# Depthwise convolution of mixer A: 124 VectorE tap operations become column-tiled TensorE products

## The chip, the cores and the metric

One Trainium2 chip, one NeuronCore of it, fp32 data. The metric is device time of one launch in microseconds (us). The kernel before was run three times: 1407.37, 1408.38 and 1410.26 us, so its median is 1408.38 us. One more execution was taken with the hardware profiler; all rows in this document come from it.

## What is computed

One layer of a hybrid decoder on 320 tokens: 256 of a prompt, then 8 sequences of 8 tokens. Cut to what matters here:

```python
def conformer_conv(a_val, a_gate, conv_prev, conv_w, conv_b, ln_g, ln_b):   # mixer A, 4 heads of 128 channels
    z = a_val * jax.nn.sigmoid(a_gate)
    zp = jnp.concatenate([conv_prev, z], axis=1)                            # 30 earlier tokens of state in front
    y = lax.conv_general_dilated(zp, conv_w[:, None, :], window_strides=(1,), padding="VALID",
                                 feature_group_count=W_A)                   # depthwise, 31 taps
    y = layernorm_heads(y + conv_b, ln_g, ln_b, N_HEADS_A)
    return jax.nn.silu(y), zp[:, -30:]                                      # the new state is an output

h = rmsnorm(x, g_mix); proj = h @ w_in                                      # 2048 x 3072
a_val, a_gate, b_u, b_v, c_u = split(proj)
out_a, conv_new = conformer_conv(a_val, a_gate, ...)                        # mixer A
out_b, v_rows   = chunk_spatial_gate(b_u, b_v, ...)                         # mixer B
out_c, hr, hi   = s5_branch(c_u, ...)                                       # mixer C, complex diagonal recurrence
x = x + concat([out_a, out_b, out_c]) @ w_out
gate, up = split(rmsnorm(x, g_ffn) @ w_gu)
x = x + (silu(gate) * up) @ w_down                                          # then a last RMSNorm
```

For a prompt the 30 earlier tokens are zeros; for the 8 sequences they come from `state_conv`.

## The kernel before

**The main stream.** Channels lie on partitions, tokens in the free dimension. All weights pass TensorE (PE) as *units* of up to 8 chunks of 128 rows. For a unit SP loads 512 KB (`raw`, L194, three buffers; `load(u + 3)` stands at the start of unit u), ScalarE (ACT) makes a rounded copy `hi` (L201), VectorE (DVE) makes the remainder `lo` (L206, a call of the helper at L55; from unit 20 on POOL makes a part of it, L209), and PE does three products per chunk: hi by the high part of the activations (L233), hi by their low part (L234), lo by the high part (L236), 24 of 128x320 per unit. The string `ORDER` sets the sequence of the input projection after heads 0 and 1 of mixer A: `C0` to `C7` are the eight output tiles of mixer C with two units each, `A2` and `A3` the gate and value tiles of heads 2 and 3, `V` the value rows of mixer B, `U0` to `U3` its gates. Then come 16 tiles of `w_out` over the rows of mixer C, 16 over those of mixers A and B, and the feed-forward part. From the end of mixer A and B on PE is busy to the end.

**The side work.** Everything else (convolution, recurrence, gating) is Python generators that the class `Side` hands out in turns between the quarters of a unit, four turns a unit, by priority and by an estimate of DVE's time against PE's. So the order of every engine's instructions is fixed when the program is built; `Wait(n)` means n turns.

**Mixer A.** `post_val` writes z of a head into a padded row `zpad0` or `zpad1` (two DVE operations at L59). `mix_a` (its lines start at L518) lets ACT copy it into `zp`, five blocks of 8 shifted columns (L524, L525), SP store the two new states (L526, L527), and DVE do the 31 taps: one multiply with bias (L65), one multiply (L64), 29 multiply-adds `ac<-zp,cw,ac` (L59) into two accumulators, one add (L55). PE subtracts the mean over channels with the matrix `cent` (L547, result `yc`); `mix_a_tail` gets the variance (PE, L557), the normed value and the activation, and ACT puts it back in token order (L568, L570).

**Mixer C.** POOL computes the parameters of the state space in a long chain of small operations that ends in `kk` (L341 to L445). DVE makes `bb` of them (`bb_task`, the operations `wv<-kk,lnv`). Per tile: `c_inputs` (POOL, L639 to L645) makes powers, PE transposes them (L720), `U` holds the inputs, reordered through DRAM by SP (`du`, L597, and L601), PE makes the states at chunk ends (L708), ACT copies them to `H` (L709). After the fourth tile `recurrence(0)` starts on half of the pairs (copy `F<-H` at L69), after the eighth `recurrence(1)`; each has 63 steps of four DVE operations of 128x32. `c_mats` and `mat_t` make the output matrices with products in four column tiles of the PE array (L820), `c_out` and `c_glu` (L892, L893) the outputs. `w_out` waits for these rows (`need_c`), its second half for all side work (`need_ab`).

Of the kernel before, what the change touches and what calls it, by code (L numbers as in the profile page):

```python
# [40 lines left out]
class Vec:  # L41
    """VectorE with a running estimate of its busy time (us)."""
# [51 lines left out]
class Side:  # L94
    """Side work, handed out between the matrix products of the main stream."""
# [21 lines left out]
    def run(self):  # L117
        """One turn: side work up to VectorE's share of the time that TensorE has been given."""
# [29 lines left out]
def _build(ctx, nc, tc, I, O):  # L148
# [30 lines left out]
    units = []  # L179

    S = {}                 # what the tasks leave for each other

    def unit(src, n, mm, cost, pre=None, post=None):
        units.append(dict(src=src, n=n, mm=mm, cost=cost, pre=pre, post=post))
# [11 lines left out]
    def split_hi(u):  # L196
        if u < len(units):
            d = units[u]
            d["hi"] = wp.tile([128, d["n"]], F32R, tag="hi", name="hi")
            for o in halves(u, d["n"]):  # L200
                A.activation(d["hi"][:, o], d["raw"][:, o], AF.Copy)  # L201

    def split_lo(u):
        if u < len(units):
# [11 lines left out]
    def tile_units(src, rows, post, need=None, psum=acc):  # L216
        """Units of one output tile: ps = W^T act over the chunks that rows() gives."""
# [37 lines left out]
    for _ in range(11):    # TensorE's clock rises with its load  # L255
        T.matmul(wps[:, 0:128], zero, zero, start=True, stop=True)
# [16 lines left out]
    cw = tmp("cw", (128, 4, 31))  # L273
# [10 lines left out]
    # zeroed once: the blocks off the diagonal and the paddings stay zero  # L284
    bds, zpads = [], []
    for i in range(2):
        b_ = tmp(f"zpad{i}", (128, 30 + NT))
        G.memset(b_[:, 0:30], 0.0)
        zpads.append(b_)
# [11 lines left out]
    def inv_sqrt(pool, var, shape, tag, neg, n=1.0):  # L301
        """(var / n + eps)^-1/2, table value and one Newton step; negated if neg. n is a power of 4."""
# [14 lines left out]
    E = G  # L317
# [77 lines left out]
    E.tensor_tensor(sp, sp, fr, op=MULT)          # sin, cos  # L395
    pw = tmp("pw", (128, 2, 5, 32))               # powers 0..4 of abar, re and im
# [26 lines left out]
    def rd_params():  # L423
        # 1 / |a|^2, with one Newton step
# [9 lines left out]
    def k_params():  # L434
        # k = (abar - 1) / a
# [72 lines left out]

    def post_val(h):
# [8 lines left out]
    def mix_a(h):  # L518
# [861 lines left out]
```

## Time and profile before

| what | value |
|---|---|
| runs, us | 1407.37, 1408.38 (median), 1410.26 |
| profiled execution, span, us | 1408.6 |
| mean granted TensorE clock | 0.97 |
| PE busy, us | 1316.6 (93%) |
| DVE busy, us | 816.4 (58%) |
| ACT busy, us | 569.1 (40%) |
| POOL busy, us | 267.8 (19%) |

The span is the time from the first to the last instruction of the profiled execution; the profile gives no other time of it. It lies 0.2 us above the median of the runs. In the rows, L12 is line 12 of the kernel before; `acc<-xh,lo` says that `acc` is written from `xh` and `lo`, with buffer numbers left out. A matrix product in full fp32 shows as two records. PEclk is the granted clock, 1.00 for 2.4 GHz.

### The profile page before, as it was taken

The numbers are of one execution on the slowest core, as the hardware profiler recorded it, in microseconds if no ns is written. First come the engines' busy times: TensorE is split into PE (matmuls) and PEld (weight loads), VectorE is DVE, ScalarE is ACT, GpSimd is POOL, SyncE is SP. The second block draws the span as 40 slices with busy tenths as digits, with TensorE's granted clock in tenths as the row PEclk, the third lists the DMA queues.
The fourth block names the chain that finished last, engine by engine and source line by source line (L and its number), as shares of the span: only waits on it lengthen the run. The fifth ranks groups of instructions, "written<-read, shape, count | busy, mean of one in ns | idle before, by whom it ended". The sixth has DMA issues, their size and how long they took to land.

```text
span 1408.6 us, 22244 instructions
## 1 busy us (share of the span) xinstructions
PE 1316.6 (93%) x8812; PEld 1292.6 (92%) x8812; DVE 816.4 (58%) x1420; ACT 569.1 (40%) x823; POOL 267.8 (19%) x364
## 2 busy tenths in 40 slices
PE   9589678798989999999999999999999999999995
PEld 9588667587889999999999999999999999999995
DVE  7398999989975544444444444444444444444444
ACT  7466434454455533333333333333333333333442
POOL 8775553446533000000000000000000000000112
PEclk9899888999999999999999999999999999999998
DMA  7253234345334444444444444444444444444443
GB/s 258 88 161 123 79 112 127 97 146 194 100 131 152 150 148 152 149 150 147 153 150 150 147 153 150 150 150 150 150 150 149 151 150 149 150 150 142 141 150 122
DMA packets 75369, 203.23 MB, mean 144 GB/s; under 512 B 17616, under 2 KB 27088, under 8 KB 75264
## 3 DMA queue, kind: packets, MB, share of 16 engines
q1 hardware_dynamic: 73472, 195.73, 42.1%
q0 software_dynamic: 1216, 4.41, 1.0%
q8 instruction: 69, 1.13, 0.3%
q10 hardware_dynamic: 576, 1.66, 0.3%
q14 instruction: 36, 0.29, 0.1%
HBM read 194.63 MB, written 7.14 MB: 143 GB/s over the span
## 4 chain that ended last, share of the span: by engine, by line
PE 72%; DVE 4%; DMA 0%; issue 0%; DVEq 0%; ACT 0%; ACTq 0%
PE acc L236 24%; PE acc L234 24%; PE acc L233 24%; DVE ac L59 2%; DVE lo L55 1%; DVE xa L55 1%; DMA xa<-in_xT 0%; DVEq L1376 0%; DVE gs L55 0%; PE sm L547 0%; DVE is L59 0%; PE sm L557 0%; PE sm L1165 0%; PE sm L1099 0%; ACT is L305 0%
## 5 line engine op out<-in xcount | busy, mean ns | idle before, releaser
L55 DVE TENSOR_TENSOR lo<-raw,hi 128x1024 fp32r<-128x1024 f32 (+2 forms) x357 | 410.1, 1150 | 209.6 <-issue 164.4
L201 ACT ACTIVATE hi<-raw 128x1024 fp32r<-128x1024 f32 (+1 forms) x357 | 365.0, 1024 | 328.4 <-PE acc L234 266.1
L233 PE MATMUL acc<-hh,hi 128*128 128x320 f32 x1408 | 424.1, 309 | 0.0
L234 PE MATMUL acc<-hl,hi 128*128 128x320 f32 x1408 | 423.1, 308 | 0.0
L236 PE MATMUL acc<-hh,lo 128*128 128x320 f32 x1408 | 320.9, 308 | 0.0
L234 PEld LDWEIGHTS acc<-hl,hi 128*128 128x128 f32 x1408 | 264.4, 188 | 0.1
L233 PEld LDWEIGHTS acc<-hh,hi 128*128 128x128 f32 x1408 | 264.2, 188 | 0.1
L236 PEld LDWEIGHTS acc<-hh,lo 128*128 128x128 f32 x1408 | 235.0, 188 | 0.0
L233 PE MATMUL acc<-fh,hi 128*128 128x320 f32 x704 | 211.9, 309 | 0.0
L234 PE MATMUL acc<-fl,hi 128*128 128x320 f32 x704 | 211.8, 308 | 0.0
L236 PE MATMUL acc<-fh,lo 128*128 128x320 f32 x704 | 165.5, 308 | 0.0
L1159 POOL COPY ss<-sq 128x320 f32<-128x320 f32 x1 | 0.5, 451 | 852.0 <-ACT sq L1155 852.0
L233 PEld LDWEIGHTS acc<-fh,hi 128*128 128x128 f32 x704 | 132.2, 188 | 0.0
L234 PEld LDWEIGHTS acc<-fl,hi 128*128 128x128 f32 x704 | 132.2, 188 | 0.0
L236 PEld LDWEIGHTS acc<-fh,lo 128*128 128x128 f32 x704 | 119.0, 188 | 0.0
L236 PE MATMUL acc<-xh,lo 128*128 128x320 f32 x288 | 71.1, 330 | 39.8 <-DVE lo L55 39.7
L55 DVE TENSOR_TENSOR xa<-acc,xa 128x320 f32<-128x320 f32 x80 | 39.2, 490 | 107.9 <-PE acc L236 107.9
L233 PE MATMUL acc<-xh,hi 128*128 128x320 f32 x288 | 94.7, 336 | 2.0 <-ACT wv L969 2.0
L209 POOL TENSOR_TENSOR lo<-raw,hi 128x512 fp32r<-128x512 f32 (+1 forms) x44 | 70.6, 1605 | 113.2 <-PE acc L236 24.6
L234 PE MATMUL acc<-xl,hi 128*128 128x320 f32 x288 | 91.2, 324 | 0.0
L236 PEld LDWEIGHTS acc<-xh,lo 128*128 128x128 f32 x288 | 51.7, 203 | 42.3 <-DVE lo L55 42.1
L1143 ACT ACTIVATE fh<-fu 128x320 fp32r<-128x320 f32 x44 | 20.8, 472 | 163.7 <-DVE fu L55 163.7
(297 smaller groups left out, 1624.8 us busy)
## 6 DMA issues: line engine op xcount, KB each, us to landing
raw<-in_wgu SPq DMA_DIRECT2D x176, 512.0 KB, 3.6
raw<-in_wdn SPq DMA_DIRECT2D x80, 512.0 KB, 3.5
raw<-in_win SPq DMA_DIRECT2D x37, 512.0 KB, 3.8
raw<-in_wout SPq DMA_DIRECT2D x32, 512.0 KB, 3.6
raw<-in_wv SPq DMA_DIRECT2D x8, 512.0 KB, 3.5
raw<-in_wdn SPq DMA_DIRECT2D x16, 256.0 KB, 2.7
xa<-in_xT POOLq DMA_DIRECT2D x4, 640.0 KB, 6.7
raw<-in_win SPq DMA_DIRECT2D x6, 256.0 KB, 6.3
```

The costliest lines, as they stand in the source:

```text
L55: return self.v.tensor_tensor(out, a, b, op=op)
L59: return self.v.scalar_tensor_tensor(out, a, s, b, op0=op0, op1=op1)
L201: A.activation(d["hi"][:, o], d["raw"][:, o], AF.Copy)
L209: G.tensor_tensor(d["lo"][:, n:], d["raw"][:, n:], d["hi"][:, n:].bitcast(F32), op=SUB)
L233: T.matmul(ps, hi[:, c], r[u + j][0], start=u + j == 0, stop=False)
L234: T.matmul(ps, hi[:, c], r[u + j][1], start=False, stop=False)
L236: T.matmul(ps, lo[:, j * 128:j * 128 + 128], r[u + j][0], start=False, stop=u + j == n - 1)
L1143: A.activation(h, ub, AF.Copy)
L1159: G.tensor_copy(s, q)
```

## The change

The 31 taps of a head become one unit of the main stream without `hi` and `lo`: `K0` to `K3`. Its 512 KB of weights (`cwd`) hold, for eight groups j of four taps and for four groups g of 32 channels, a 128x32 block whose four 32x32 parts are diagonal, one part per tap. Its input `z4` holds the padded row four times per channel group, shifted by 0 to 3 tokens, so that partitions are (shift, channel). A head then takes 8 x 4 products over the 256 prompt columns and 8 x 4 over the 64 sample columns, each group g into its own column tile of the PE array. The shifted rows are made by writing the padded row (128x596) to DRAM (`zr`, SP) and reading four pieces back (SP); the prompt's and the samples' parts lie in one row with their 30 columns of state in front, which SP now loads from `state_conv` directly into the row. The two output states are stored from the row by POOL's queue.

```diff
-ORDER = "C0 C1 C2 C3 C4 C5 C6 C7 A2 U0 U1 A3 V U2 U3".split()
+ORDER = "C0 C1 K0 C2 C3 K1 C4 C5 C6 C7 A2 U0 U1 K2 A3 V K3 U2 U3".split()
+ZS, ZW, Z4 = 288, 596, 592
 def post_val(h):
     def f(ps):
         side.until(lambda: h < 2 or ("zp", h - 2) in S)
-        z = zpads[h % 2][:, 30:30 + NT]
-        V.scalar_tensor_tensor(z, ps, 0.5, S["rstd"], op0=MULT, op1=MULT)
-        V.scalar_tensor_tensor(z, S["gs", h], 1.0, z, op0=ADD, op1=MULT)
-        side.add(5.5 + 0.1 * h, mix_a(h))
+        row, gs = zpads[h % 2], S["gs", h]
+        V.scalar_tensor_tensor(gs, gs, 1.0, ps, op0=ADD, op1=MULT)
+        V.scalar_tensor_tensor(row[:, 30:286], gs[:, 0:NP], 0.5, S["rstd"][:, 0:NP], op0=MULT, op1=MULT)
+        V.scalar_tensor_tensor(samples(row)[:, :, 30:38], gs[:, NP:]..., 0.5, S["rstd"][:, NP:]..., op0=MULT, op1=MULT)
+        side.add(0.3, conv_in(h))
+def state_load(h):
+    nc.sync.dma_start(samples(zpads[h % 2])[:, :, 0:30], I["sconv"][h].rearrange("p (s t) -> p s t", s=8))
+def conv_in(h):
+    row = zpads[h % 2]
+    dz = dp.tile([128, ZW], F32, tag="zr", name="zr")
+    yield Wait(2)
+    nc.sync.dma_start(dz, row)
+    nc.gpsimd.dma_start(O["ncp"][h], row[:, 256:286])
+    nc.gpsimd.dma_start(O["ncs"][h].rearrange("p (s t) -> p s t", s=8), samples(row)[:, :, 8:38])
+    S["zp", h] = True
+    yield Wait(4)
+    z4 = S["z4", h] = tmp("z4", (128, 4, Z4))
+    base = dz[0:1, 0:1]
+    for g in range(4):
+        nc.sync.dma_start(z4[:, g], bass.AP(tensor=base.tensor, offset=base.offset + 32 * g * ZW,
+                                            ap=[[1, 4], [ZW, 32], [1, Z4]]))
+    if h < 2:
+        yield Wait(1)
+        state_load(h + 2)
+def k_mm(h):
+    def f(w, i):
+        ps, z4 = S["k", h], S["z4", h]
+        o, n = (0, NP) if i < 3 else (NP, 64)
+        taps = ((0, 1, 2), (3, 4, 5), (6, 7), range(8))[i]
+        for j in taps:
+            for g in range(4):
+                c = slice(32 * g, 32 * g + 32)
...
+                T.matmul(ps[c, o:o + n], w[:, 32 * (8 * g + j):32 * (8 * g + j) + 32], x,
+                         start=j == 0, stop=j == 7, tile_position=(0, 32 * g))
+def k_post(h):
+    def fn():
...
+        A.activation(f, S["k", h][:, :NT], AF.Identity, bias=cv[:, h, 0:1])
+        side.add(0.9, mix_a(h, f))
 def mix_a(h, f):
...
     T.matmul(yc[:, :NT], cent, f, start=True, stop=True)
```

`z4` has one buffer, `raw` keeps three, and a K unit calls `load(u + 3)` at its end instead of its start. The states of heads 0 and 1 are loaded at unit 2, those of heads 2 and 3 behind the `z4` reads of heads 0 and 1. The load of the taps (`cw`) goes; the bias rows of mixer B (`bs`) are loaded later, into the tile of `bb`; the residual rows `xa` are loaded by `post_u(3)` at the latest; POOL clears four more small stretches at the start.

Three places in the order of instructions, each before and after. The first is SP's queue around the first two heads (`zr_694`, `zr_695`, `z4_748`, `z4_753` are the rows and pieces of heads 0 and 1, `raw_670` the weights of K0, `raw_720` and `raw_771` those of the two units of C2, `raw_890` the first of C3). Before, `raw_706` and `raw_756` are the second unit of C2 and the first of C3:

```order
L194 DMA raw_706<-in_win 128x1024 [waits DMAHW1_49,DMAHW4_49,DVE_49,Activation_49]
L523 DMA zp_734<-in_sconv 128x240
L526 DMA out_ncp<-zpad0_121 128x30
L527 DMA out_ncs<-zp_734 128x240 [waits DMAHW5_49,Activation_49]
L597 DMA du_711<-zc_709 128x320 [waits DVE_49]
L194 DMA raw_756<-in_win 128x1024 [waits DMAHW2_49,DVE_49]
L194 DMA raw_795<-in_win 128x1024 [waits DMAHW3_49,DVE_49]
```

After (the pieces of one head are four rows alike, the first is shown; `zpad0` and `zpad1` are the states of heads 2 and 3, and they wait for two DMAs of POOL's queue, DMASW):

```order
L191 DMA raw_720<-in_win 128x1024 [waits DMAHW2_49,DVE_49,Activation_49]
L616 DMA du_725<-zc_723 128x320 [waits DVE_49]
L531 DMA z4_748<-zr_694 128x1x592 [waits DMAHW5_49]
...
L531 DMA z4_753<-zr_695 128x1x592 [waits DMAHW3_49,DMAHW4_49,DMAHW2_49,DMAHW6_49,DMAHW1_49,PE_49]
...
L516 DMA zpad0_120<-in_sconv 128x8x30 [waits DMASW2_49]
L516 DMA zpad1_124<-in_sconv 128x8x30 [waits DMASW4_49]
L191 DMA raw_771<-in_win 128x1024 [waits DVE_49]
L616 DMA du_725<-zc_808 128x320 [waits DVE_49]
L191 DMA raw_890<-in_win 128x1024 [waits DMAHW5_49,DVE_49]
```

Ahead of the first unit of C3 stood three DMAs of head 0 and the store of a C tile; now the eight reads and two state loads stand ahead of C2's second unit already, and the weights of C3 behind that. Those two DMAs of POOL's queue are the stores `out_ncs`, and in POOL's order they come behind `kk`:

```order
L442 TENSOR_TENSOR wv_138<-wv_138 128x32 [waits Pool_49]
L443 TENSOR_TENSOR kk_260<-wv_138,r10_261 128x32 [waits Pool_49]
L524 DMA out_ncp<-zpad0_120 128x30 [waits DVE_49]
L525 DMA out_ncs<-zpad0_120 1024x1x30 [waits DMAHW4_49,DVE_49]
L524 DMA out_ncp<-zpad1_124 128x30 [waits DVE_49]
L525 DMA out_ncs<-zpad1_124 1024x1x30 [waits DMAHW5_49,DVE_49]
L637 DMA wv_849<-in_h0 128x512 [waits DVE_49,Pool_49]
L711 MEMSET H_884 128x64 [waits PE_49,Activation_49]
```

Of these rows the four stores are new on POOL; the load of `in_h0` stood directly behind `kk` before. On ACT the copy `hi_812` of C2's second unit (from `raw_771`) stands now ahead of two `bbd` copies and of K0's result:

```order
L198 ACTIVATE hi_773<-raw_720 128x1024 [waits DMAHW7_49,PE_49]
L198 ACTIVATE hi_812<-raw_771 128x1024 [waits DMAHW3_49,DVE_49,PE_49]
L830 ACTIVATE bbd_132<-bb_781 64x8x16 [waits DVE_49,Pool_49]
L830 ACTIVATE bbd_132<-bb_781 64x8x16
L564 ACTIVATE of_894<-acc_814,cv_106 128x320 [waits PE_49]
L198 ACTIVATE hi_898<-raw_890 128x1024 [waits DMAHW5_49]
L668 ACTIVATE bd0_128<-t1_907 64x4x3x16 [waits Pool_49]
```

PE takes `of_894` (for `yc`) behind the third quarter of C2's first unit, so what moved is that this quarter's end now depends on the weights of the unit after it. DVE's `lo` of C2's first unit stands behind the operations on `kk` now, as that of its second unit did before. The second place is DVE up to the start of the first recurrence (`F<-H`). Before:

```order
L59 SCALAR_TENSOR_TENSOR ac_785<-zp,cw,ac_785 128x320
L55 TENSOR_TENSOR ac_785<-ac_785,ac_786 128x320
L55 TENSOR_TENSOR zc<-acc,rs 128x320
L55 TENSOR_TENSOR lo<-raw,hi 128x1024 x2
L65 TENSOR_SCALAR ac_1298<-zp,cw,cv 128x320
L64 TENSOR_SCALAR ac_1299<-zp,cw 128x320
L59 SCALAR_TENSOR_TENSOR ac_1298<-zp,cw,ac_1298 128x320
L59 SCALAR_TENSOR_TENSOR ac_1299<-zp,cw,ac_1299 128x320
L59 SCALAR_TENSOR_TENSOR ac_1298<-zp,cw,ac_1298 128x320
L59 SCALAR_TENSOR_TENSOR ac_1299<-zp,cw,ac_1299 128x320
L55 TENSOR_TENSOR zc<-acc,rs 128x320
L55 TENSOR_TENSOR lo<-raw,hi 128x1024
L69 COPY F<-H 128x2x144
L69 COPY H<-wv 128x2x16x8
L55 TENSOR_TENSOR r_1365<-a4r,H 128x32
```

After:

```order
L52 TENSOR_TENSOR zc<-acc,rs 128x320
L52 TENSOR_TENSOR lo<-raw,hi 128x1024
L56 SCALAR_TENSOR_TENSOR is_986<-sm,is_986 128x320
L56 SCALAR_TENSOR_TENSOR is_984<-is_986,is_984 128x320
L52 TENSOR_TENSOR is_984<-sm,is_984 128x320
L56 SCALAR_TENSOR_TENSOR of<-of,is_984 128x320
L52 TENSOR_TENSOR zc<-acc,rs 128x320
L52 TENSOR_TENSOR lo<-raw,hi 128x1024 x3
L52 TENSOR_TENSOR zc<-acc,rs 128x320
L52 TENSOR_TENSOR lo<-raw,hi 128x1024
L56 SCALAR_TENSOR_TENSOR is_1323<-sm,is_1323 128x320
L56 SCALAR_TENSOR_TENSOR is_1321<-is_1323,is_1321 128x320
L52 TENSOR_TENSOR is_1321<-sm,is_1321 128x320
L66 COPY F<-H 128x2x144
L66 COPY H<-wv 128x2x16x8
L52 TENSOR_TENSOR r_1439<-a4r,H 128x32
L52 TENSOR_TENSOR r_1440<-a4i,H 128x32
```

The taps are gone; between them and the recurrence stand only `lo`, `zc` and the tail of head 1 (`is`, `of`). `F<-H` is row 67 instead of row 100. The second copy `F<-H`, which starts the other recurrence, comes behind 53 steps of the first instead of behind 45, so of the 63 steps of each 10 stand among those of the other instead of 18. The third place is PE behind the last unit of C3:

```order
L233 MATMUL acc<-xh,lo 128x320 x2
L555 MATMUL acc<-z_753,raw 32x256 x32
L555 MATMUL acc<-z_753,raw 32x64 x32
L727 MATMUL sc<-U,P 128x80 x8
L739 MATMUL sc<-ident,bd_128 128x128 x8
L230 MATMUL acc<-xh,hi 128x320
L231 MATMUL acc<-xl,hi 128x320
L230 MATMUL acc<-xh,hi 128x320
L231 MATMUL acc<-xl,hi 128x320
L233 MATMUL acc<-xh,lo 128x320 x2
...
L573 MATMUL sm<-of,cent 128x320
...
L581 MATMUL sm<-of,ones_113 128x320
```

K1 stands there as two rows of 32 products, then the chunk-end states of the second C tile (L727) and the transposes of the third (L739), then, three quarters and five quarters of a unit later, the mean and the variance of head 1 (L573, L581). The L708 or L727 products of the fourth C tile, which release the first recurrence, stand 7.5 weight units behind the first product of C2's second unit before, and 7 weight units and K1 behind the first product of C2's first unit after.

## Rows read from the trace of the kernel before

**Rows 1.** The page, busy time: us (share of the span) and instructions of each engine

```profile
PE 1316.6 (93%) x8812; PEld 1292.6 (92%) x8812; DVE 816.4 (58%) x1420; ACT 569.1 (40%) x823; POOL 267.8 (19%) x364
```

**Rows 2.** Stretches: length, busy (xcount) of PE, PEld, DVE, ACT, POOL; PEclk, DMA, GB/s

```profile
75.00:116.00 41.00, 36.93 (x271) 35.79 (x271) 36.08 (x47) 30.24 (x63) 30.17 (x39) 1.00 0.51 160
116.00:180.00 64.00, 45.34 (x316) 43.30 (x315) 61.14 (x198) 28.03 (x56) 35.92 (x46) 0.90 0.27 83
...
285.00:406.00 121.00, 105.92 (x641) 99.66 (x641) 108.91 (x181) 62.81 (x91) 60.05 (x47) 0.93 0.43 141
406.00:1393.00 987.00, 985.52 (x6721) 985.10 (x6720) 457.05 (x548) 361.91 (x445) 32.24 (x31) 1.00 0.45 148
```

**Rows 3.** PE's waits, 75 to 116 us: us in total, times, longest

```profile
PE sm L547 <- DVE ac L55: 1.7, 1, 1.7
```

**Rows 4.** The same view, 285 to 406 us

```profile
PE acc L236 <- DVE lo L55: 9.5, 4, 3.5
PE acc L233 <- ACT wv L969: 2.0, 1, 2.0
```

**Rows 5.** Stretches of the tile `ac` alone: PE, PEld, DVE busy (xcount)

```profile
75.00:116.00 41.00, 0.81 (x2) 0.30 (x2) 23.80 (x35) 1.00 0.51 160
116.00:180.00 64.00, 0.00 (x0) 0.00 (x0) 0.00 (x0) 0.90 0.27 83
...
285.00:406.00 121.00, 2.71 (x6) 1.13 (x6) 61.12 (x90) 0.93 0.43 141
```

**Rows 6.** Timeline around 70 us: start, duration, instruction, [idle before, releaser]

```profile
65.92 0.25 POOL L445 TENSOR_TENSOR kk<-wv,r 128x32 f32<-128x32 f32 x1
...
71.12 0.33 SPq L194 DMA_DIRECT2D raw<-in_win  x1
71.15 0.90 PE L236 MATMUL acc<-xh,lo 128*128 128x320 f32 x2 [15.23 <-DVE lo L55]
...
72.52 0.63 ACT L811 ACTIVATE bbd<-bb 64x128 f32<-64x128 f32 x2 [15.83 <-DVE bb L55]
...
73.00 0.65 POOL L618 DMA_DIRECT2D wv<-in_h  x1 [6.83 <-DVE ac L64]
...
73.17 1.06 ACT L201 ACTIVATE hi<-raw 128x1024 fp32r<-128x1024 f32 x1
```

**Rows 7.** DMA issues: engine, count, KB each, median us from issue to landing

```profile
raw<-in_win SPq DMA_DIRECT2D x37, 512.0 KB, 3.8
...
craw<-in_s5c POOLq DMA_DIRECT2D x8, 64.0 KB, 2.5
```

**Rows 8.** Timeline of PE at 203 us

```profile
203.28 0.66 PE L820 MATMUL sc<-bd,bbd 128*32 128x128 f32 x16
203.88 0.42 PE L233 MATMUL acc<-xh,hi 128*128 128x320 f32 x1
```

**Rows 9.** Line L892: ns min/median/max, first and last start

```profile
L892 PE MATMUL sc<-zc,wg x16: 430/432/508, 243.4 to 323.8; 128*128 128x320 f32 x16
```

**Rows 10.** Timeline of DVE: the recurrence's start, one step, a step of both, the end

```profile
115.89 0.31 DVE L69 COPY F<-H 128x288 f32<-128x288 f32 x1 [1.97 <-ACT H L709]
...
117.19 0.22 DVE L55 TENSOR_TENSOR r<-a4r,H 128x32 f32<-128x32 f32 x1
...
117.95 0.22 DVE L55 TENSOR_TENSOR r<-a4r,H 128x32 f32<-128x32 f32 x1
...
182.28 0.21 DVE L55 TENSOR_TENSOR r<-a4r,H 128x32 f32<-128x32 f32 x1
...
183.27 0.21 DVE L55 TENSOR_TENSOR r<-a4r,H 128x32 f32<-128x32 f32 x1
...
284.61 0.42 DVE L55 TENSOR_TENSOR F<-lnv 128x256 f32<-128x256 f32 x1
```

**Rows 11.** Timeline of PE at the start of the last `w_out` half

```profile
408.45 0.41 PE L234 MATMUL acc<-ol,hi 128*128 128x320 f32 x1 [1.48 <-DVE ol L55]
```

More of the change, by code (lines that the diff above doesn't have):

```diff
@@ L181, in _build, with unit @@
     S = {}
-    def unit(src, n, mm, cost, pre=None, post=None):
-        units.append(dict(src=src, n=n, mm=mm, cost=cost, pre=pre, post=post))
+    def unit(src, n, mm, cost, pre=None, post=None, whole=False):
+        units.append(dict(src=src, n=n, mm=mm, cost=cost, pre=pre, post=post, whole=whole))
     def halves(u, n):
@@ L196, in split_hi @@
     def split_hi(u):
-        if u < len(units):
+        if u < len(units) and not units[u]["whole"]:
             d = units[u]
@@ L203, in split_lo @@
     def split_lo(u):
-        if u < len(units):
+        if u < len(units) and not units[u]["whole"]:
             d = units[u]
@@ L507, in post_gate, with samples @@
         return f
+    def samples(row):
+        return row[:, ZS:ZS + 304].rearrange("p (s t) -> p s t", s=8)
     def post_val(h):
@@ new lines, in k_pre, with f @@
+    def k_pre(h):
+        def f():
+            side.until(lambda: ("z4", h) in S)
+            S["k", h] = acc()
+        return f
+    def k_mm(h):
[6 more added lines that the diff above has]
+                    c = slice(32 * g, 32 * g + 32)
+                    if i < 3:
+                        x = z4[:, g, 4 * j:4 * j + NP]
+                    else:
+                        x = z4[:, g, ZS:ZS + 304].rearrange("p (s t) -> p s t", s=8)[:, :, 4 * j:4 * j + 8]
+                    T.matmul(ps[c, o:o + n], w[:, 32 * (8 * g + j):32 * (8 * g + j) + 32], x,
+                             start=j == 0, stop=j == 7, tile_position=(0, 32 * g))
+        return f
@@ L548, in mix_a, with mix_a_tail @@
         side.pe += 0.53
-        S["conv", h] = True
-        side.add(3, mix_a_tail(h, yc))
-    def mix_a_tail(h, yc):
-        sq = tmp("sqa")
-        A.activation(sq, yc[:, :NT], AF.Square)
+        side.add(3, mix_a_tail(h, yc, f))
+    def mix_a_tail(h, yc, o):
+        A.activation(o, yc[:, :NT], AF.Square)
         yield Wait(2)
         var = sm()
-        T.matmul(var[:, :NT], ones128, sq, start=True, stop=True)
+        T.matmul(var[:, :NT], ones128, o, start=True, stop=True)
         side.pe += 0.53
@@ L975, in b_task @@
         yield Wait(2)
-        while "lnv" not in S:
+        while "lnv" not in S or "bs" not in S:
             yield Wait(1)
@@ L1179, in _build @@
             a_tiles(int(t[1]))
+        elif t[0] == "K":
+            h = int(t[1])
+            unit(I["cwd"][h], 1024, k_mm(h), 5.1, k_pre(h), k_post(h), whole=True)
         elif t[0] == "C":
@@ L1225, in _build @@
     for u, d in enumerate(units):
-        load(u + 3)
+        if not d["whole"]:
+            load(u + 3)
         if u < 2:
@@ L1248, in _build @@
         if u == 1:
-            for t, n in ((cv, "cv"), (bgl, "bgl"), (dsk, "dsk"), (cw, "cw")):
+            for t, n in ((cv, "cv"), (bgl, "bgl"), (dsk, "dsk")):
                 nc.sync.dma_start(t, I[n])
@@ L1262, in _build @@
             nc.sync.dma_start(bld, I["s5b"])
+            state_load(0)
+            state_load(1)
         if u == 16:
@@ L1277, in _build @@
         for i in range(4):
-            d["mm"](d["hi"], d["lo"], n * i // 4, n * i // 4 + n // 4)
+            if d["whole"]:
+                d["mm"](d["raw"], i)
+            else:
+                d["mm"](d["hi"], d["lo"], n * i // 4, n * i // 4 + n // 4)
             side.pe += d["cost"] / 4
             side.run()
+        if d["whole"]:
+            load(u + 3)
         for k in ("raw", "hi", "lo", "mm", "pre", "post"):
```

81 lines of the change are left out of this document (31 added, 50 removed).

## The prediction, made before the changed kernel ran

> **What bounds the kernel now.** I read the page first. PE is busy for 93% of the span, DVE for 58% [rows 1], so taking work from DVE pays only where DVE holds PE up. The view by stretches tells where. From 406 us on PE runs 6721 records in 987 us, 0.147 us each, with 985.5 us busy [rows 2]: nothing in that part is touched, and it only moves earlier or later as a whole. The question is therefore when the weight stream reaches that part, and the change works on four stretches ahead of it.
>
> *Up to 71 us* PE stands still for 15.2 us: it needs `lo` of C2's second unit, DVE is held by `kk`, and POOL's parameter chain delivers that at 66.2 [rows 6]. No tap is involved. *From 71 to 116 us* PE is nearly full (36.9 of the 41 us from 75 on), though 23.8 us of taps lie on DVE there [rows 2, 5]. PE waited for a tap result once, 1.7 us [rows 3]. The recurrence starts at 115.89, released over ACT by PE's chunk-end products [rows 10]. *From 116 to 285 us* DVE is the bound (61.1 of the first 64 us busy) and PE has room (45.3 of 64) [rows 2]. The change takes nothing away here: the tile `ac` has no operation there at all, 0.00 in the stretch shown and in the two that follow it to 285 [rows 5]. The recurrence ends at 284.61 [rows 10]. *From 285 to 406 us* 61.1 us of taps fall on DVE [rows 5], and PE is busy for 105.9 of 121 us at a mean clock of 0.93 [rows 2]. Of its 15.1 us of waits 9.5 are for `lo` [rows 4]. So of the 84.9 us of taps in the two stretches [rows 5] only about 11 hold up PE directly.
>
> **The change, part by part**, in us against the profiled span of 1408.6 (0.2 above the median of the runs).
>
> *Price of a K unit.* The nearest row is the column-tiled product L820: 8 products of 128 columns take 0.60 from their start to the next full product, with both changes of array layout [rows 8]. A head has ten times those columns (32 products of 256, 32 of 64): 6.0 if every tenth pays the changes again. It pays them at its ends alone, so I take 5.5. The far end is no overlap of the four tiles: a full fp32 product of 320 columns has records of 0.43 [rows 9], and 32 of these make 13.8.
>
> The Trainium skill, TensorEngine Tiling (Array Packing), Key Properties, says that a change of tiling mode drains TensorE, while its tiles run independently. The row agrees with the second and makes the first small (0.60 for both changes and the eight products). TensorE: Matmul & The Clock Gate, Measured speedup vs the span model, gives a speedup of 2.38 for three column tiles; by that a head would be an estimated 13.8/2.38 = 5.8, and the sum would be 0.6 higher for K1 and K3 together. No run so far shows three.
>
> *K0: 0.* It needs no `lo`, so it runs inside the 15.2 us for which PE stands still. Bounds: 0, and 5.5 if its rows came back from DRAM after 66 us. A write to DRAM and a read back are 2.5 to 3.8 each by the nearest rows [rows 7], so pieces asked for by 60 are in time.
>
> *71 to 116 us: +5.5.* The order on SP and POOL makes a new chain. POOL issues four state stores behind `kk`: 66.2 + 4 x 0.65 (the issue of L618) = 68.8, 2.5 to land as `craw` does: 71.3. SP's two state loads wait for them (0.33 each, as the issue at 71.12, twice that if many short runs cost more: 72.3), and C2's second weights come only then: + 3.8 = 76.1. ACT copies them (1.06), then two `bbd` (0.63), then K0's result (a third of the columns of `hi`, about 0.5): 78.3 [rows 6, 7]. PE meanwhile does the 14 products left of three quarters of C2's first unit from 71.15 on, at 0.147 or, after standing still, at up to twice that, and then needs K0's result for `yc`: at 73.2 to 75.3, of which I take 74.8. That is a wait of 3.5, new. Then K1 in full, 5.5, since PE is the bound here. Against it: the wait of 1.7 for the taps goes, and from the stall to the fourth tile's chunk-end products it is 7 weight units instead of 7.5 (-1.8; a unit is 24 x 0.147 = 3.5). 3.5 + 5.5 - 1.7 - 1.8 = 5.5, and the recurrence starts at about 121.5. Bounds: +1, if the stores land early enough for no wait and half of K1 falls into other waits of PE, and +12, if each store of 1024 short runs costs POOL two or three times the row's 0.65.
>
> *116 to 285 us: +4.9.* DVE is the bound, and what hides K2 is PE's room. By the order 8 more of the 63 steps of each recurrence run alone. A step alone takes 0.76, a step of both together 0.99 [rows 10], so each pair of lone steps costs 2 x 0.76 - 0.99 = 0.53 more: 8 x 0.53 = 4.2. A third operation for the padded row, and some `lo` pulled in, add 0.7. Bounds: 0, if other DVE work fills the gaps of lone steps, and 8.
>
> *285 to 406 us: -9.0.* Without taps PE is the bound. The waits for `lo` go, 9.5. The mean clock of 0.93 means 121 x 0.07 = 8.5 of lost work, part of it in the idle time itself; I take 5.0 back. K3 stands in this stretch: + 5.5. The other 5.6 of waits stay: they are for ACT, a weight of the GLU and the value rows (2.0 of them [rows 4]), which no tap delays. Bounds: -15 (full clock and the other waits gone too) and -3 (K3's own waits and no clock).
>
> *After 406 us: -1.5.* The one wait of 1.48 at 408.45 for a row of `ol` from DVE [rows 11] goes, as DVE is no longer late. Bounds 0 and -1.5.
>
> *At no cost:* the ACT copies of `zp` and of the rows back to token order go (ACT is busy for 62.8 of 121 us [rows 2]); 305 KB per head of rows written and 1.2 MB read lie beside a DMA share of 0.27 to 0.51 [rows 2]; the loads of states at unit 2 delay early weights by less than the stall of 15.2 absorbs; loads of `bs` and `xa` are not awaited at their places. If that cover went, about one weight load, 3.8 [rows 7], would show.
>
> Sum: 0 + 5.5 + 4.9 - 9.0 - 1.5 = -0.1, so **1408.5**. No change, within 0.2% (2.8 us), which is about what a measurement of this kernel can tell.
>
> **The rivals.**
>
> *A, the late start does not come and the end closes up (faster).* The four stores land before PE needs K0's result (-3.5), the clock stays at its upper level after 285 us (-3.5), and 4 of the other 5.6 of waits vanish in a stream that DVE no longer delays: 1408.5 - 11 = 1397.5. For it: all slack on DVE after 285 us. Against it: POOL cannot issue before 66.2 [rows 6], and those waits are for ACT and DMA.
>
> *B, the taps count in full (faster by far).* If DVE were the bound wherever taps lie, 23.8 + 61.1 would go [rows 5] and 11 for two K units come: 1408.6 - 84.9 + 11 = 1335. Against it: PE's own 36.9 of 41 and 105.9 of 121 [rows 2].
>
> *C, POOL's queue (slower).* Each state store is 1024 runs of 120 bytes. If the four take POOL 9 instead of 2.6, C2's second weights start 6.4 later and so does everything to the recurrence, and K3, whose result passes ACT behind the value rows, keeps PE waiting for 4 more: 1408.5 + 10 = 1418.5. It decides from the point at which the last store lands later than 71.3: every us behind that is one on the time, since PE has nothing else to do. For it: SP's weights queue behind those stores by order. Against it: the issues by POOL that the trace shows are cheap, 0.65 for one of 128 rows [rows 6].
>
> *D, the tiles do not overlap (slower).* A head then takes 13.8, K1 and K3 add 8.3 each: 1425. Against it stands the 0.60 of [rows 8].
>
> **How the numbers follow.** The forecast's case, 1403 to 1414, has 0.47; two of its terms have bounds wider than 2.8, so 0.29 of it is no change, 0.08 faster, 0.10 slower. A has 0.26, B 0.02, C 0.21, D 0.04. Faster: 0.26 + 0.02 + 0.08 = 0.36; same 0.29; slower: 0.21 + 0.04 + 0.10 = 0.35. The range leaves out B, D and the outer parts of A and C: 1395 to 1421. The bounds of any single term, from -6.0 to +6.5 about its value, lie inside it.
>
> **What would show it.** Right: K0 inside the stall; PE waiting 3 to 4 us at the first `yc` with ACT's K0 result as releaser, and SP's state loads waiting for POOL's stores; `F<-H` at 119 to 124; the recurrence's end at 293 to 297 with DVE full between; then a dense PE, about 112 us to the last half of `w_out`, and 5 to 6 us for a K unit. Wrong: a recurrence that starts before 117 (A) or after 127 (C), K units over 8 us (D), or PE waits of over 10 us after the recurrence, in which case something other than the taps had held PE there.

## The result and the profile after

The changed kernel takes 1447.84 us (median of 4 runs, 1446.54 to 1451.24) against 1408.89 (4 runs of the kernel before beside it, 1407.37 to 1410.26). The ratio is 1.0277, with a 95% interval of 1.0261 to 1.0294: slower by about 39 us, where no change was predicted and 1421 was the upper end of the range.

The page's busy times after, against [rows 1]:

```profile
PE 1338.0 (93%) x9324; PEld 1300.5 (90%) x9324; DVE 751.0 (52%) x1296; ACT 559.5 (39%) x812; POOL 270.1 (19%) x378
```

DVE has lost 65.4 us of work and PE has gained 21.4, which is 5.4 for each of four heads. So the work itself is what it was priced at. Where the time went is told by stages. The view of the tile `F` gives the start and the end of the recurrence (first and last start stand behind the three durations):

```profile
L66 DVE COPY F<-H x2: 303/400/498, 137.6 to 205.0; 128x288 f32<-128x288 f32 x2
L52 DVE TENSOR_TENSOR F<-lnv x2: 412/418/425, 240.9 to 321.3; 128x256 f32<-128x256 f32 x2
```

The recurrence starts at 137.6 instead of 115.89 [rows 10] (+21.7), lasts 183.7 instead of 168.7 (+15.0), and from its end to the end of the span it is 1125.1 instead of 1124.0 (+1.1). Together that is the 37.8 between the spans, 1446.4 and 1408.6. Of the three the first is to be found in the view of PE's waits up to 460 us (us in total, times, longest):

```profile
PE acc L233 <- DVE lo L52: 27.7, 9, 5.4
PE sm L573 <- ACT of L564: 20.5, 1, 20.5
PE acc L977 <- ACT gs L964: 12.1, 3, 6.4
PE sc L839 <- ACT m L674: 8.0, 1, 8.0
PE acc L555 <- DMA z<-zr: 7.5, 4, 2.4
```

The second row is the wait for K0's result at the first `yc`. It was forecast at 3.5 us and is 20.5. It empties the stretch that was nearly full [rows 2]; by stretches, with the columns of [rows 2]:

```profile
75.00:116.00 41.00, 21.85 (x166) 19.60 (x170) 9.11 (x11) 19.48 (x40) 14.05 (x20) 0.71 0.50 146
```

The mean granted clock is 0.71 there, where it was 1.00: PE stands still for half of the stretch and is granted less than its upper level for part of it. Who is behind that wait is shown by the chain that ended last (start, us, what), of which these pieces lie between 49 and 95 us, and two later:

```profile
49.31 13.62 DMA z<-zr
62.98 7.76 PE acc L555 x121
72.67 1.50 SPq L531
74.84 10.19 SPq L516
85.08 6.40 DMA raw<-in_win
93.77 1.43 PE sm L573 x2
...
209.56 14.05 DMA dk<-kpad
...
299.71 12.78 DMA dk<-kpad
```

The reads of `z4` of head 0 take 13.6 us. K0 on PE follows, and since `z4` has one buffer, the reads of head 1 wait for it, with SP standing at them (SP's view of waits):

```profile
SPq L531 <- PE acc L555: 7.7, 1, 7.7
```

Behind those reads SP's own issue of a state load (L516) takes 10.19 us, and only then does it issue the weights of C2's second unit. SP's timeline (start, us, instruction) shows the same, one queue held by 1.2 MB per head:

```profile
47.43 26.74 SPq L531 DMA_DIRECT2D z<-zr  x8
74.21 10.82 SPq L516 DMA_DIRECT2D zpad<-in_sconv  x2
85.08 3.17 SPq L191 DMA_DIRECT2D raw<-in_win  x1
```

An issue on SP was 0.33 us in [rows 6]. Those weights were due at 76.1 by the prediction. ACT has them at 91.59, and K0's result stands behind them on ACT, as the order said. How fast the reads are can be seen in the stretch in which little else moves:

```profile
49.40:62.80 13.40, 6.07 (x32) 3.96 (x30) 0.00 (x0) 1.06 (x1) 11.30 (x44) 0.85 0.28 110
```

A DMA share of 0.28 and 110 GB/s: about four of sixteen engines. The piece `z4[:, g]` has the four shifts as its outermost dimension. The Trainium skill, DMA: Bandwidth & Descriptors, Why a DMA increments its semaphore by 16 and not by 1, says that a transfer is spread over the largest number of engines up to 16 that divides the slowest dimension of both sides, so four here; the trace agrees, with its 0.28.

### The profile page after: what moved, and what is told of

Same layout as the page of the kernel before. It is cut to its first block, busy times and chain, and to the rows that moved or that the text cites. A ratio compares the mean times of both kernels' runs of the same rounds, so it can differ in the third digit from the quotient of the medians.

```text
span 1446.4 us, 23194 instructions
## 1 busy us (share of the span) xinstructions
PE 1338.0 (93%) x9324; PEld 1300.5 (90%) x9324; DVE 751.0 (52%) x1296; ACT 559.5 (39%) x812; POOL 270.1 (19%) x378
## 4 chain that ended last, share of the span: by engine, by line
PE 80%; DVE 11%; DMA 4%; ACT 2%; SPq 1%; issue 1%; DVEq 0%; ACTq 0%
PE acc L233 25%; PE acc L230 25%; PE acc L231 25%; DVE r L52 5%; DVE H L52 2%; DMA dk<-kpad 2%; PE acc L555 1%; DVE lo L52 1%; DMA z<-zr 1%; SPq L516 1%; DMA dz<-z 0%; DVE ol L52 0%; DMA raw<-in_win 0%; ACT hi L198 0%; DMA x<-in_xT 0%
## 5 line engine op out<-in xcount | busy, mean ns | idle before, releaser
L52 DVE TENSOR_TENSOR lo<-raw,hi 128x1024 fp32r<-128x1024 f32 (+2 forms) x357 | 415.8, 1166 | 255.5 <-issue 170.3
L198 ACT ACTIVATE hi<-raw 128x1024 fp32r<-128x1024 f32 (+1 forms) x357 | 365.3, 1024 | 371.8 <-PE acc L231 260.8
L206 POOL TENSOR_TENSOR lo<-raw,hi 128x512 fp32r<-128x512 f32 (+1 forms) x46 | 74.0, 1611 | 97.9 <-PE acc L233 53.7
L1145 ACT ACTIVATE fg<-fg 128x320 f32<-128x320 f32 x44 | 20.7, 472 | 138.6 <-DVE fg L52 138.6
```

What stands on the lines that cost most here:

```text
L52: return self.v.tensor_tensor(out, a, b, op=op)
L206: G.tensor_tensor(d["lo"][:, n:], d["raw"][:, n:], d["hi"][:, n:].bitcast(F32), op=SUB)
L1145: A.activation(gs, gs, AF.Silu)
```

## The experiments

Each was run beside the kernel before; ratios are to that, with 95% intervals. A summary by stages, from the view of `F` in each profiled execution:

| kernel | recurrence starts, us | lasts, us | from its end on, us | median, us | ratio |
|---|---|---|---|---|---|
| before | 115.9 | 168.7 | 1124.0 | 1408.89 | |
| after | 137.6 | 183.7 | 1125.1 | 1447.84 | 1.0277 |
| `e1_spread` | 128.0 | 174.5 | 1127.1 | 1427.80 | 1.0138 |
| `e2_late_state` | 137.0 | 184.1 | 1123.7 | 1447.03 | 1.0274 |
| `e3_both` | 121.8 | 173.0 | 1123.6 | 1423.39 | 1.0107 |
| `e5_no_taps` | 110.2 | 168.4 | 1106.5 | 1385.95 | 0.9839 |
| `e6_interleave` | 119.6 | 173.5 | 1129.1 | 1421.95 | 1.0091 |
| `e7_k1_late` | 118.3 | 170.0 | 1124.3 | 1414.16 | 1.0039 |
| `e8_pace` | 117.2 | 182.9 | 1109.4 | 1412.46 | 1.0026 |
| `e9_all_late` | 112.3 | 167.7 | 1132.3 | 1413.92 | 1.0041 |
| `e10_k3_early` | 112.0 | 163.3 | 1140.7 | 1418.29 | 1.0069 |
| `e11_k_free` | 112.5 | 180.1 | 1114.6 | 1409.48 | 0.9996 |
| `e12_k_free_pace` | 112.2 | 186.7 | 1113.4 | 1415.19 | 1.0046 |
| `e13_few_taps` | 111.2 | 174.5 | 1114.1 | 1405.09 | 0.9970 |

### The late start: reads or state loads

**e1_spread**: one read per shift into 32 partitions, all four groups at once.

```diff
-        for g in range(4):
-            nc.sync.dma_start(z4[:, g], bass.AP(... offset + 32 * g * ZW, ap=[[1, 4], [ZW, 32], [1, Z4]]))
+        for s in range(4):
+            nc.sync.dma_start(z4[32 * s:32 * s + 32], bass.AP(... offset + s, ap=[[ZW, 32], [32 * ZW, 4], [1, Z4]]))
```

> The changed kernel with the four reads of z4 cut by shift (32 partitions times 4 channel groups) instead of by channel group (4 shifts times 32 channels); the bytes and runs are the same. Theory 1 (a read whose outermost dimension is 4 is served by 4 of the 16 DMA engines, about 100 GB/s in the profile, and everything behind it on SP's queue waits): a read lands in 1 to 1.5 us instead of 3, K0 runs closed up, the wait for K0's result at the first yc falls from 20.5 us to 5 to 10, the 14 us of the store of kpad around 210 us fall under 5; time 1415 to 1430. Theory 2 (the state loads behind POOL's stores hold SP's queue, as rival C of the prediction has it): 1443 to 1450, the wait stays near 20.

**e2_late_state**: the state loads of heads 2 and 3 leave the place ahead of C2's second weights.

```diff
-            yield Wait(1)
+            yield Wait(16)
             state_load(h + 2)
```

> The changed kernel with the loads of the states of heads 2 and 3 sixteen turns after the z4 reads instead of one turn. Theory 1 (the reads on 4 engines hold SP's queue): the weights of C2's second unit are issued at 74 instead of 85 us but queue behind the reads on those 4 engines, so the wait at the first yc is still 12 to 18 us; time 1440 to 1447. Theory 2 (the state loads are what holds the queue): the wait falls below 8 us; time 1428 to 1436.

**e3_both**: both edits.

> Both edits together: z4 reads cut by shift, and state loads of heads 2 and 3 sixteen turns later. Theory 1: the remaining part of the wait at the first yc (POOL's stores, which land at about 74 us) goes as well: wait 0 to 4 us, F<-H at 118 to 122, time 1405 to 1417. Theory 2: the same as the run with late state loads alone, 1428 to 1436.

Measured: `e1_spread` 1427.80, ratio 1.0138 (1.0122 to 1.0155); `e2_late_state` 1447.03, 1.0274 (1.0258 to 1.0289); `e3_both` 1423.39, 1.0107 (1.0090 to 1.0124). The wait at the first `yc` is 11.8, 21.8 and 4.2 us. Theory 1 has the direction each time, but not all sizes: it expected these waits at 5 to 10, 12 to 18 and 0 to 4 us, and `e3_both` at 1405 to 1417. The reads of `e1_spread` run at a share of 0.83:

```profile
49.40:57.00 7.60, 3.84 (x27) 3.58 (x25) 0.00 (x0) 1.06 (x1) 6.35 (x23) 1.00 0.83 195
```

With the state loads alone moved, SP's queue backs up all the same, now at what stands behind the reads: the weights are issued at 73.38, but the next issue takes 6.22 us and ACT copies them at 92.10 (`e2_late_state`, timelines of SP and of ACT):

```profile
73.38 1.00 SPq L191 DMA_DIRECT2D raw<-in_win  x1
74.43 6.22 SPq L616 DMA_DIRECT2D du<-zc  x1
```

```profile
92.10 1.06 ACT L198 ACTIVATE hi<-raw 128x1024 fp32r<-128x1024 f32 x1 [40.19 <-DMA raw<-in_win]
```

So the slow reads are the first cause: moving the state loads gains nothing as long as they are there, and 4.4 us once they are spread (by medians; the profiled execution of `e1_spread` is the slowest of its four). What remains in `e1_spread` is a second, smaller cause, which its chain shows:

```profile
65.86 0.54 POOL out_ncp L524
66.41 11.32 DMA out_ncs<-zpad
77.74 0.55 SPq L516
78.33 4.62 DMA raw<-in_win
```

POOL issues its stores in time and cheaply, but the last one, 1024 runs of 120 bytes, has landed at 77.7 only, 11.32 us from the start of its issue. The recurrence of `e3_both`, where nothing waits for it, starts 6.2 earlier.

### What the taps had cost

**e5_no_taps** is the kernel before without 116 of its 124 tap operations, in the same order of instructions.

```diff
-                V.scalar_tensor_tensor(ac[k % 2], src, w, ac[k % 2], op0=MULT, op1=ADD)
+                V.t += 0.129 + 0.00104 * NT
```

> The kernel before with 29 of the 31 taps of each head left out (116 of 124 operations on DVE), every other instruction in the same place; nothing takes their place, so it shows what the taps held up. The prediction's reading (the waits for lo and ac of 11 us, some 5 us of clock, 1.5 at the end): 1386 to 1397. The rival that the taps count in full: 1325 to 1335. If they held nothing up: 1406 to 1409.

Measured: 1385.95 against 1409.57, ratio 0.9839 (0.9814 to 0.9864): 23.6 us, of 84.9 of DVE time [rows 5]. By stages 5.7 lie ahead of the recurrence, 0.3 in it, 17.5 behind it. For 140 us from its end on the view of PE's waits has three rows left:

```profile
PE sc L892 <- DMA wg<-in_wglu: 2.1, 1, 2.1
PE acc L233 <- ACT wv L969: 2.0, 1, 2.0
PE acc L234 <- DVE ol L55: 1.5, 1, 1.5
```

Of the 5.7 ahead, 1.7 are not the taps': POOL's `kk` ends at 64.52 instead of 66.17 in this execution, and the first tap comes only behind it. The rest is the 1.7 for `ac` [rows 3] and one more wait of PE between 75 and 116 us that is gone with the taps:

```profile
PE sc L720 <- POOL g L641: 2.0, 1, 2.0
```

So about 22 us are the gain that a change of this kind has to divide with its own costs. `e4_no_taps`, an earlier form that also took the taps out of the builder's account, gave no time.

### How fast the reads can be

**e6_interleave**: `e2_late_state` with the partitions as (channel, shift), so that the outermost dimension is 32 and all 128 partitions are written; the weights `cwd` are arranged to fit.

```diff
-                                                ap=[[1, 4], [ZW, 32], [1, Z4]]))
+                                                ap=[[ZW, 32], [1, 4], [1, Z4]]))
```

> The changed kernel with the late state loads, and with z4's partitions as (channel, shift) instead of (shift, channel), the weights laid out to match: each of the four reads of a head has outermost dimension 32 and still goes to all 128 partitions, where the reads cut by shift went to 32 partitions each. Theory 1a (those were held by the narrow destination: 127 GB/s at a DMA share of 0.58): the four reads of a head land within 4 to 6 us of the first issue instead of 10, the wait at the first yc is under 2 us, F<-H at 117 to 120, time 1413 to 1420. Theory 1b (runs shifted by 4 bytes are slow on the DRAM side, whatever the cut): as the run with both edits, 1420 to 1426.

Measured: 1421.95, ratio 1.0091 (1.0060 to 1.0122). The first 3.6 us of the reads, and K0 on PE, without the four waits for pieces:

```profile
49.40:53.00 3.60, 3.60 (x26) 3.60 (x26) 0.00 (x0) 1.06 (x1) 2.92 (x9) 1.00 0.96 357
```

```profile
54.01 5.46 PE L555 MATMUL acc<-z,raw 128*32 128x256 f32 x128
```

The reads are now fast and the wait at the first `yc` is gone, as theory 1a has it. The time lies in the range of theory 1b: it is only 1.4 below that of `e3_both`, and the intervals overlap. Up to 125 us PE now waits 10.0 us for `lo`, where it waited 6.1 in `e3_both`: K0 ends earlier, but that stall, which DVE's operations on `kk` set, ends at 70.25 as it did at 69.54. The 128 records are the 64 products of a head, in 5.46 us: the price of a K unit.

### Where the K units stand

**e7_k1_late**: `e6_interleave`, K1 behind all tiles of mixer C, so out of the way to the recurrence's start.

```diff
-ORDER = "C0 C1 K0 C2 C3 K1 C4 C5 C6 C7 A2 U0 U1 K2 A3 V K3 U2 U3".split()
+ORDER = "C0 C1 K0 C2 C3 C4 C5 C6 C7 K1 A2 U0 U1 K2 A3 V K3 U2 U3".split()
```

> The run before this one with K1 moved in the stream from behind C3 to behind C7, into the first recurrence. If PE is the bound up to the fourth tile's chunk-end products (the prediction's step of 5.5 for K1): F<-H 4 to 6 us earlier, the recurrence's end and the time 4 to 6 us less than there. If another wait takes its place or DVE refills the stretch: no change, within 2 us.

Measured: 1414.16, ratio 1.0039 (1.0025 to 1.0053), 7.8 less. In the profiled execution only 1.3 of the difference is at the recurrence's start, 3.5 in it and 4.8 behind it. So the size is above the 4 to 6 expected and the place is another. At the start the room of K1 is partly filled again: 160 products of `lo` pass ahead of it for 152, one weight unit more. Why the rest is gained later is not shown.

**e9_all_late** and **e10_k3_early**: `e6_interleave` with all four K units inside the recurrence's stretch or behind it, and a head's reads waiting for the K unit before.

```diff
-ORDER = "C0 C1 K0 C2 C3 K1 C4 C5 C6 C7 A2 U0 U1 K2 A3 V K3 U2 U3".split()
+ORDER = "C0 C1 C2 C3 C4 C5 C6 C7 K0 A2 U0 K1 A3 U1 K2 V U2 K3 U3".split()    # e9_all_late
+ORDER = "C0 C1 C2 C3 C4 C5 C6 C7 K0 A2 K1 U0 A3 K2 U1 U2 K3 V U3".split()    # e10_k3_early
...
+        while h and ("k done", h - 1) not in S:
+            yield Wait(1)
```

> The run with z4 as (channel, shift) and late state loads, with ORDER changed to C0 to C7, K0, A2, U0, K1, A3, U1, K2, V, U2, K3, U3, and the reads of the next head's z4 behind the K unit of the head before. K0 to K2 then stand in the stretch of the recurrence, where PE is idle for 39 of 170 us; K3 stays behind it. If the products cost only where PE is the bound (reading of the runs so far: the run without taps shows what is left, 1386): F<-H at 109 to 113, the recurrence's stretch 168 to 176 us, about 5 for K3 behind it, time 1390 to 1402, ahead of the kernel before. If the K units lengthen the recurrence (their waits for z4, ACT and the tails' operations on DVE): 1405 to 1416.

> The same with the order C0 to C7, K0, A2, K1, U0, A3, K2, U1, U2, K3, V, U3, so that all four K units and two U tiles stand ahead of the value rows. By the same reading K3 is hidden too, and the 10 to 14 us of waits at the value rows, which come later, shrink: 1386 to 1400. If PE's idle time in the recurrence belongs to the value rows' own waits, moving the rows behind the recurrence lengthens the end instead: 1400 to 1415.

Measured: 1413.92, ratio 1.0041 (1.0024 to 1.0058), and 1418.29, 1.0069 (1.0048 to 1.0091). Both miss a gain. The time of `e9_all_late` lies in the range of its second case, but not for that case's reason, since the recurrence has not grown. The start is at 112.3 and 112.0, ahead of the kernel before, and the recurrence is as short as there or shorter, yet the stretch behind it has grown by 8.3 and 16.7. The products that take `lo`, eight to a weight unit, tell why (kernel before, then `e9_all_late`; PE's busy time and count on the tile `lo` during the recurrence and behind it):

```profile
115.89:284.60 168.71, 49.04 (x163) 0.88 0.34 104
284.60:1408.60 1124.00, 558.80 (x2409) 0.99 0.44 148
```

```profile
112.30:280.00 167.70, 37.37 (x136) 0.84 0.44 124
280.00:1412.30 1132.30, 567.60 (x2436) 0.99 0.47 150
```

The builder hands out side work by an account of PE's time; a K unit stands in it with 5.1 us. What K units take of the recurrence's stretch, weight units do not get: 27 products, 3.4 units of 3.5 us, move behind it.

### The account

**e8_pace**: `e7_k1_late`, each DVE operation of 32 elements estimated 0.06 us higher, so that more weight units pass in the recurrence.

```diff
-        self.t += fixed + per * n
+        self.t += fixed + per * n + (0.06 if n == 32 else 0)
```

> The run before this one with the builder's estimate of a DVE operation of 32 elements raised by 0.06 us, so that the recurrence is spread over more weight units. If what is paid after the recurrence is set by the weight units that the order leaves there (23.2 in the changed kernel, 21.8 before, each 3.5 us of PE that is idle during the recurrence): units left fall by 2 to 5, the recurrence's stretch grows by under 1 us per unit, the time falls by 5 to 12 us. If the recurrence's stretch grows by as much as is taken away: within 2 us.

Measured: 1412.46, ratio 1.0026 (1.0011 to 1.0041). Behind the recurrence 14.9 us go; in it 12.9 come, so it is the second case. Of the 12.9 DVE's view of waits puts 9.8 down to a single wait (for rows of `zc` from DRAM), so this run does not show what the spreading alone costs.

**e11_k_free**: `e9_all_late`, the K units at no cost in the account. **e12_k_free_pace**: the same with 0.03 more per small operation.

```diff
-            unit(I["cwd"][h], 1024, k_mm(h), 5.1, k_pre(h), k_post(h), whole=True)
+            unit(I["cwd"][h], 1024, k_mm(h), 0.0, k_pre(h), k_post(h), whole=True)
...
-        self.t += fixed + per * n
+        self.t += fixed + per * n + (0.03 if n == 32 else 0)    # e12_k_free_pace alone
```

> The run with all K units late, with a K unit counted as 0 instead of 5.1 us of TensorE time in the builder's account, by which DVE's side work is let forward. There 24.8 weight units were left at the end of the recurrence, against 21.8 before. If the account is the cause (15 us counted for three K units that TensorE does in its idle time): 21.5 to 22.5 units left, the recurrence's stretch up to 3 us longer, time 1400 to 1407, ahead of the kernel before. If the units are left for another reason: 1411 to 1416.

> The same, with the estimate of a DVE operation of 32 elements raised by 0.03 us as well, half of what was tried. If the stretch of the recurrence still has room for weight units at under 2 us each: 20 to 21 units left, 2 to 4 us less than the run before this. If each further unit lengthens the recurrence by what it saves: the same within 2 us.

Measured: `e11_k_free` 1409.48 against 1409.17, ratio 0.9996 (0.9984 to 1.0009), equal to the kernel before; `e12_k_free_pace` 1415.19, 1.0046 (1.0028 to 1.0065), a miss. In `e11_k_free` the units are back (2411 products behind the recurrence), but the recurrence is 12.4 longer than in `e9_all_late`; it was expected to grow by 3 at most, and the time fits neither case. DVE now waits for PE in that stretch:

```profile
DVE lo L52 <- PE acc L233: 6.8, 3, 3.4
DVE lo L52 <- PE acc L981: 5.9, 1, 5.9
```

In `e9_all_late` the two rows are 2.1 and 2.2, so 8.4 of the 12.4 can be these waits: DVE's order is fixed, and each holds the steps of the recurrence behind it. DVE's own work in the stretch is 6.1 longer too (161.6 us busy for 155.5), as more weight units pass there.

**e13_few_taps**: `e11_k_free` with 6 of the 8 groups of taps left out of each K unit.

```diff
-            taps = ((0, 1, 2), (3, 4, 5), (6, 7), range(8))[i]
+            taps = ((0,), (), (7,), (0, 7))[i]
```

> The run with all K units late and counted as 0, with 6 of the 8 tap groups of every K unit left out (16 of 64 products stay), every other instruction in the same order: what the products themselves cost in their places, about 4 of 5 us each. If TensorE's room in the recurrence hides K0 to K2 (the prediction's reading of that stretch), only K3 shows: 3 to 5 us less. If the two engines, each in its own order, wait for each other there so that TensorE's time is paid in the main: 9 to 14 us less, and the recurrence's stretch falls from 180 to about 171.

Measured: 1405.09 against 1408.90, ratio 0.9970 (0.9957 to 0.9984), 4.4 below `e11_k_free`. PE is busy with the products of the K units for 5.6 us instead of 18.6, and these 13 us are worth 4.4: most of them are covered. The size is that of the first case, the place is not: in the profiled executions the recurrence is 5.6 shorter and the stretch behind it, where K3 stands, 0.5. It is still 19 above `e5_no_taps`. Of the 14.7 between the profiled executions 6.1 lie in the recurrence and 7.6 behind it; these runs do not separate what that is (the loads of K's weights, the pieces of the tails, the order).

## Why the prediction was wrong, step by step

**The reading of the kernel before holds in the main.** The taps count where they hold up PE and not in full: at most 23.6 of 84.9 us. The sum had credited 1.7 ahead of the recurrence and 9.5 + 5.0 + 1.5 = 16.0 behind it; `e5_no_taps` shows 5.7, of which 4.0 are the taps', and 17.5. What the sum missed ahead is mostly the wait for POOL's `g`. Rival B (1335) counted on the naive sum and lies 51 us below even that kernel.

**The price of a K unit holds.** 5.5 was taken; 5.46 were measured for K0 closed up (`e6_interleave`), and 4.56 for K1 in the kernel after:

```profile
113.30 4.56 PE L555 MATMUL acc<-z,raw 128*32 128x256 f32 x128
```

Rival D needed 13.8 and falls. That price was itself too low: it counts one record of 0.43 for a product, and in the kernel before two full products of 320 columns start 0.54 apart, so 32 make 17.3:

```profile
243.39 0.70 PE L892 MATMUL sc<-zc,wg 128*128 128x320 f32 x2
243.93 0.70 PE L893 MATMUL sc<-zc,wg 128*128 128x320 f32 x2
```

The Trainium skill, TensorEngine Tiling (Array Packing), Key Properties, states that a change of mode drains TensorE; in 4.56 us for 64 products there is no room for more than a small price of it.

**The step that failed is "A write to DRAM and a read back are 2.5 to 3.8 each by the nearest rows, so pieces asked for by 60 are in time".** The price came from rows of `raw` and `craw` [rows 7], whose outermost dimension is 128 partitions. The pieces of `z4` have four there. They take 13.6 us per head, and were then put down as lying "beside a DMA share of 0.27 to 0.51": bytes were weighed and not engines. K0 itself still ran in PE's stall, as forecast, with 7.5 us of waits for its pieces. The cost came at the next step, whose chain has no term for the reads that stand on SP's queue ahead of C2's weights.

**"71 to 116 us: +5.5" was +21.7.** The chain named there is the right one, down to ACT's copy of K0's result behind C2's second weights. Two sizes in it were wrong. The reads on SP's queue ahead of those weights cost 9.6 (137.6 to 128.0, `e1_spread`). And a store of 1024 short runs lands not 2.5 us after its issue "as `craw` does": it costs 6.2 (128.0 to 121.8, `e3_both`). With both gone the start is at 121.8, where the prediction had put it at 121.5, and the wait at `yc` is 4.2 against its 3.5. That agreement is luck. The 3.5 hung on POOL's stores, for which nothing waits in `e3_both`; its 4.2 come from C2's weights, which its chain shows landing 11.11 us after their issue, behind the reads of head 1:

```profile
64.45 11.11 DMA raw<-in_win
```

In `e6_interleave`, with faster reads, this wait is gone. Rival C had the direction and the second of these: a last store landing 6.4 later than 71.3, with a price of 6.4, where `e1_spread` shows 77.7 and 6.2. But it sought the delay in POOL's issue, which is cheap; it lies in the landing. In the kernel after, this cost is hidden beside the reads, as `e2_late_state` shows.

**"116 to 285 us: +4.9" was +15.0.** The kernel without the two delays has +4.3. The other part is again the reads: those of heads 2 and 3 stand on SP ahead of the store of `kpad`, whose pieces in the chain are 14.05 and 12.78 us (SP's timeline for head 2):

```profile
206.66 2.80 SPq L531 DMA_DIRECT2D z<-zr  x4
209.56 4.22 SPq L861 DMA_DIRECT2D dk<-kpad  x1
```

In the kernel before this store landed 1.8 to 4.9 us after its issue. ACT writes the next `kpad` only then, and DVE stands behind it; the view of DVE's waits in the recurrence has this row in the kernel after, then in `e1_spread`, and none in the kernel before:

```profile
DVE kpad L56 <- ACT kpad L851: 8.5, 2, 6.6
```

```profile
DVE kpad L56 <- ACT kpad L851: 1.3, 1, 1.3
```

In `e1_spread` one piece is left in the chain, 9.77 where under 5 was expected, and the stretch is 9.2 shorter. The remaining +4.3 is near the forecast in number, but no run varies the lone steps, so that they are its cause is not shown.

**"285 to 406 us: -9.0" and "After 406 us: -1.5" were +1.1, and -0.4 in `e3_both`.** Removing the two delays gives nothing back here, so this is a second error. PE's busy time and idle time from the recurrence's end on, before and in `e3_both`:

```profile
284.60:1408.60 1124.00, 1093.18 (x7367) 1085.48 (x7366) 574.92 (x736) 426.75 (x539) 96.53 (x79) 0.99 0.44 148
```

```profile
294.80:1418.40 1123.60, 1098.47 (x7535) 1088.26 (x7534) 534.40 (x642) 417.11 (x527) 97.29 (x81) 0.99 0.45 149
```

Idle time falls from 30.8 to 25.1, so 5.7 and not the 11.0 that were credited: of the waits for `lo` one of 5.4 is left, and `sm` waits for ACT's `of`, K's own. Busy time grows by 5.3 and not by 0.5 (K3 less 5.0 of clock). Here the sum contradicts itself: it credited 1.8 for fewer weight units ahead of the recurrence and never charged them behind it. The products that take `lo`, ahead of the recurrence in the kernel before, then ahead of it, in it and behind it in `e3_both`:

```profile
0.00:115.90 115.90, 38.51 (x164) 0.93 0.51 170
```

```profile
0.00:121.80 121.80, 36.52 (x152) 0.93 0.66 186
121.80:294.80 173.00, 46.52 (x163) 0.87 0.43 120
294.80:1418.40 1123.60, 561.15 (x2421) 0.99 0.45 149
```

As many units as before pass in the recurrence (163 products), 12 fewer ahead of it, so 12 more are left behind it, 2421 for 2409. That is 1.5 units, 5.3 us. K3's 5.5 and these 5.3 leave 5.5 less for all else, which is near the 5.0 credited to the clock.

**What this leaves of the change.** With the reads spread, the stores out of the way and the K units placed and booked otherwise, it is level with the kernel before (`e11_k_free`) and not better. By stages it starts the recurrence 3.4 earlier, spends 11.4 more in it and 9.4 less behind it. What is won ahead and behind is spent in the recurrence, and of the 17.5 that the taps had cost behind it 9.4 are had. None of the versions that computes all taps beats the kernel before. No run gave `z4` a second buffer or its reads another queue, so what these would win is open.

## What to carry to other kernels

Before pricing a DMA by the nearest row, compare the outermost dimension of its access pattern with that row's, and then read what stands behind it in the same issuing queue: the slow transfer itself was covered here, and the weights behind it were not. Work that a stream leaves undone ahead of a stage comes back behind it, so units must be counted in every stage and sum to the same number. Moving work from a slack engine to the one that bounds the span pays only for the part that had held up that engine, here at most 23.6 of 84.9 us, and what is added to the bounding engine must be smaller.

## What was not expected of the hardware

- In the stretches shown, other traffic included, the reads with an outermost dimension of 4 moved 110 GB/s at a DMA share of 0.28, those with 32 into 32 partitions 195 GB/s at 0.83, and those with 32 into 128 partitions 357 GB/s at 0.96. From 51 to 53 us, in the midst of the reads, the second kind (`e3_both`) moved 217 GB/s and the third (`e6_interleave`) 403, at the same share of 1.05 by the view: half as much at a full share. The two differ in the partitions that a read fills and in the order of the rows in DRAM; no run here separates why.
- SP's issue of a state load, 0.59 us at the shortest, took 10.19 us behind eight reads with an outermost dimension of 4. In `e2_late_state`, with another DMA in that place, it took 6.22: it is the queue, not the instruction.
- POOL's store of 1024 runs of 120 bytes costs 0.9 to 1.0 us to issue and lies on the chain of `e1_spread` with 11.32 us, against 2.5 for a `craw` load of half its size [rows 7].
